# Later sums of weights, attention spills on ScalarE's queue, and four chunks first in a two-layer diffusion block

## The chip, the cores and the metric

One Trainium2 chip, one of its cores. The metric is the device time of one execution in microseconds, the median of several runs. TensorE (PE) multiplies, ScalarE (ACT) and VectorE (DVE) work elementwise, GpSimd (POOL) and SyncE (SP) mostly issue DMAs here. Each engine takes its instructions strictly in the order in which the program has them.

## The reference, cut to what matters

512 latent tokens and 256 context tokens of width 1024 go through two layers, in float32. A layer is

```python
h = modulate(rms_norm(x, norm1_g[l]), sh1, sc1)
glu, q, k, v, rq, rk, rv, rg, gates = split(h @ w_in[l] + b_in[l])
a   = conv_module(glu, ...)                    # depthwise convolution of 31 taps, layer norm
att = latent_attention(q, k, v, k_c, v_c)      # 8 heads, 2 key/value heads
ret = retention_output(bidir_retention(rq, rk, rv, ...), rg, ...)
y   = merge_branches(gates, a, att, ret, w_pa, w_pb, w_pc) @ w_out[l]
x   = x + g1 * y
gt, val = split(modulate(rms_norm(x, norm2_g[l]), sh2, sc2) @ w_up[l])
x   = x + g2 * ((silu(dwconv(gt)) * val) @ w_down[l])
```

The context tokens take the same path in layer 0 only (768 tokens there, 512 in layer 1). sh, sc and g come from the conditioning through `w_ada`.

## The kernel before

**Products.** A float32 operand is split into a high and a low part (`whi`, `wlo` for weights, `hh`, `hl` for activations), and a block of 128x128 weights takes three matmuls: `hh,whi`, `hl,whi`, `hh,wlo`. Weights come as one stream of tiles `raw` of 512 KB or less, loaded on SP's queue (L199, six buffers); ACT makes `whi` of each (L218), DVE `wlo` (L219).

**Feed-forward of layer 0.** `w_up` is not multiplied as it stands. For each of 22 chunks (`c`) the four blocks 11, 12, 21, 22 are combined in seven products on half of the tokens (384): 11, 12, S2, S1, S3, 22, S4. S1 to S4 are sums of the weights' blocks. They are made in DRAM, in six batches of four chunks (the last of two), by `make_sums`: per batch four copies (L627, 1 MB each, half of it in the last batch) and four accumulating DMAs (L632), all issued by POOL. Of a batch S1 = 21 + 22, S3 = 11 + 21, S2 = 11 + S1, S4 = 12 + S2, so that an S2 waits for an S1 and an S4 for an S2. `make_sums` is called after six steps of `ORDER[0]`, named in `SUMAT`, with a whole batch each; only its four copies have a dependency on the last matmul of the step.

**The mixers.** `ORDER` gives the steps of a layer: K, Q0, R0 and so on. Attention (`mixers`) runs beside them in four units of two heads each. A unit scores in PSUM tiles `ps`, takes exponentials on ACT (`prob`, L1361), turns them by PE (L1378), copies them to SBUF on ACT (`probt`, L1379), multiplies by `vt` (tile `ps<-probt,vt`), and leaves its result in a tile `att` (ACT, L1393). A complete `att` is written to DRAM (`attsp`) by `spill` (L1497) on POOL's queue, since nearly all tiles share 45 slots of SBUF; its slot can be used again when the write has landed. After the attention one load on POOL's queue (L1583) brings `ij`, from which retention's decay tables are made (`kdec` L916, `dec` L930 on ACT, and DVE behind them), and `kb` (L981).

**POOL's order.** In layer 0 the queue holds, one behind the other: sums, spills of attention, the load of `ij`, and behind the last sum the loads of `rowa` (L588) and `crow` (L574), with which DVE computes modulations (`crowt` L577, L599).

**From the mixers to the feed-forward.** `last_chunks` multiplies by `w_out`, the last four output chunks on one half of the tokens and then on the other. While the second half runs, the generator `split_tokens` advances the norm of the first half, a fixed number of steps per chunk. `up_seven` then begins with the products 11 and 12 of chunks 0 to `UPFIRST`-1, which need the first half alone. S2 needs both halves: the norm's `rstd`, then on DVE `b` (L708), `t` (L744, L745), then `hh` on ACT (L716) and `hl` on DVE (L717). ACT and DVE evacuate the products into `fg` (L1732, L1737) in the same stretch.

Of the kernel before, what the change touches and what calls it, by code (L numbers as in the profile page):

```python
# [18 lines left out]
F32 = mybir.dt.float32  # L19
F32R = mybir.dt.float32r  # L20
AF = mybir.ActivationFunctionType
ALU = mybir.AluOpType
# [3 lines left out]
P = 128  # L26
D = 1024
KC = D // P
# [9 lines left out]
NUP = 74  # L38
# [8 lines left out]
ORDER = ('K Q0 R0 Q1 A R1 G0 C G1 G2 G3 P0 P1 P2 P3 T T T T',  # L47
         'K Q0 Q1 R0 A G0 C R1 G1 G2 G3 P0 P1 P2 P3 T T T T T T')
ATT_LEAD, RET_LEAD = (3, 2), (1, 1)
ATTR, RETR, CONVR, ADAR = (1.0, 1.0), (1.4, 1.6), (0.4, 0.4), (0.06, 0.28, 0.4, 0.33)  # L50
SUMAT = ("R1", "G1", "G2", "G3", "P1", "P2")
QLAG = 2
HOLDO, HOLDD = (4, 4), (4, 6)
LEADO, LEADD, LEADB = 2, 2, ((0, 0, 0), (4, 0, 4))
# [15 lines left out]
HALF = TALL // 2  # L70
EVEN = [(0, HALF), (HALF, HALF)]
Q = 4 * P
# [22 lines left out]

UPFIRST = 3
CUTS = ((0, 4), (4, 8), (8, 12), (12, 16), (16, NFF))
CUTAT = {5: 0, 9: 1, 13: 2, 17: 3}  # L100

# [1 line left out]
def up_order():  # L103

    first = range(UPFIRST)
    out = [(n, c) for c in first for n in ("11", "12")] + [(n, c) for n in ("S2", "S1", "S3") for c in first]
    for c in range(UPFIRST - 1):
        out += [("22", c), ("S4", c)]
    for c in range(UPFIRST, NFF):
        out += [("11", c), ("22", c - 1), ("S4", c - 1)]  # L110
        if c in CUTAT:
            out.append((CUTAT[c],))
        out += [("12", c), ("S2", c), ("S1", c), ("S3", c)]
    return out + [("22", NFF - 1), ("S4", NFF - 1)]
# [3 lines left out]
BLOCKS = ("11", "12", "21", "22")  # L118

SUMS = (("S1", "21", ("22",)), ("S3", "11", ("21",)), ("S2", "11", ("S1",)), ("S4", "12", ("S2",)))  # L120


def batches():
    return [range(c, min(c + BATCH, NFF)) for c in range(0, NFF, BATCH)]
# [14 lines left out]
def parts(segs):  # L139

    if len(segs) > 1:
        return [[s] for s in segs]
    n = segs[0][1] // 2
    return [[(0, n)], [(n, n)]]
# [140 lines left out]
class Kern:  # L285
# [90 lines left out]
        self.cost = n * 3 * sum(c for _, c in segs) * 0.000425  # L376
        return pts

    def last_chunks(self, key, xs, segs, hold, evac, norm, lead=0, limit=None):

        n = len(xs)
        if lead:
            for m, pts in enumerate(self.group([lambda k, m=m: key(m, k) for m in range(lead)], xs, segs)):
                evac(m, pts)
            self.tick(self.cost)
        for m in range(lead, KC - hold):
            evac(m, self.dense(lambda k: key(m, k), xs, segs))
            self.tick(self.cost)  # L390
        self.W.keep(P)
        if limit:
            self.W.limit = limit
        ws, tiles = [], []
        for m in range(KC - hold, KC):
            ws.append([])
            for k in range(n):
                ws[-1].append(self.W.next(key(m, k), P))
                if k == 0:
                    tiles.append(self.W.cur)  # L400
        tiles.append(self.W.cur + (self.W.off == SUB))
        gen = None
        halves = parts(segs)[::-1] if limit else parts(segs)
        for i, hs in enumerate(halves):
            for j, m in enumerate(range(KC - hold, KC)):
                evac(m, self.dense(None, xs, hs, ws[j]))
                if i == len(halves) - 1:
                    ws[j] = None
                    self.W.release(tiles[j + 1])
                if gen:  # L410
                    for _ in range(1 + KC // hold):
                        next(gen, None)
                self.tick(self.cost)
            if gen:
                for _ in gen:
                    pass
            gen = norm(hs)
        self.W.release()
        return gen
# [198 lines left out]
        t = self.up_sums[b][name] if name in self.up_sums[b] else self.io[f"wup{4 * b + BLOCKS.index(name)}"]  # L618
        return t[:, j * Q:j * Q + Q]

    def make_sums(self, b):

        n = len(batches()[b]) * Q
        src = {x: self.io[f"wup{4 * b + i}"] for i, x in enumerate(BLOCKS)}
        for name, base, more in SUMS:
            t = src[name] = self.up_sums[b][name] = self.dram.tile([P, n], F32, name=f"sum{name}_{b}")
            first = self.nc.gpsimd.dma_start(t, src[base], max_dma_last_dim=2048)  # L627

            info = mybir.DependencyInfo(mybir.DependencyClass.Sync, mybir.DependencyReason.DATA)
            self.tc.add_manual_dep(first.ins, self.last_mm.ins.name, info, reason="later")  # L630
            for x in more:
                self.nc.gpsimd.dma_start(t, src[x], accum_op=ALU.add, max_dma_last_dim=2048)  # L632


    def rstd2(self, pts, name, y=None):

# [857 lines left out]
            nc.vector.tensor_tensor(merged[m][:, :w], merged[m][:, :w], th[:, :w], op=ALU.add)  # L1494

    def spill(self, dst, t, w):
        self.nc.gpsimd.dma_start(dst[:, :w], t[:, :w])  # L1497

    def reload(self, src, n, w):
        out = []  # L1500
# [54 lines left out]
    def layer_mixers(self, l, last, segs, T, xs, xsp, first, h2):  # L1555
        nc, io = self.nc, self.io
# [11 lines left out]
        def scaled(gen, rate):  # L1568
            for us in gen:
                yield None if us is None else us / rate  # L1570

        def mixers():
            def ready(hp):
                if hp == 0:
                    self.finish(qk["K"], qk["Q0"])
                if hp == 2:
                    self.finish(qk["Q1"])
                self.att_done = hp
            yield from scaled(self.att_gen(nt, ready), ATTR[l])
            self.att_done = 4  # L1580
            self.qq = self.kk = self.vt = None
            self.ij = self.S("ij")
            nc.gpsimd.dma_start(self.ij[:, :4 * P + 2], io["ij"])  # L1583
            self.ret_tables()
            for p in range(4):
                while self.ret_in[p] is None:
                    yield None
                a, self.ret_in[p] = self.ret_in[p], True
                yield from scaled(self.ret_gen(p, *a, not last), RETR[l])
                self.ret_done += 1  # L1590
            self.rvt = self.rv = self.ij = None
        us = [None] * 4
        ths, merged = [], [None] * KC
        for step in ORDER[l].split():
            kind, i = step[0], int(step[1:] or 0)
            if kind == "K":
                qk[step] = self.side(self.kv_unit(first.pop(0) if first else None))
            elif kind == "Q":
                qk[step] = self.side(self.q_unit(i, nt, first.pop(0) if first else None))
            elif kind == "R":  # L1600
                self.rv_unit(i)
            elif kind == "A":
                mix = self.side(mixers())
            elif kind == "G":
                us[i] = self.glu(i, segs, T)
            elif kind == "C":
                conv = self.side(self.conv_gen(us, segs), CONVR[l])
            elif kind == "P":
                while self.att_done < min(4, i + ATT_LEAD[l]) or self.ret_done < i - RET_LEAD[l]:
                    mix.step()  # L1610
                self.ret_in[i] = self.ret_inputs(i, segs, T)
            elif kind == "T":
                ths.append(self.gate(2, len(ths), segs))
            if l == 0 and step in SUMAT:
                self.make_sums(SUMAT.index(step))
        self.finish(mix)
        if l == 0:
            self.finish(ada)
# [26 lines left out]
        def evac(m, pts):  # L1645
            for pt, o, c in kinds(pts):
# [4 lines left out]

        norm = self.norm(l, 1, xs, h2) if last else self.split_tokens(l, xs, h2)
        return self.last_chunks(lambda m, k: ("w_out", l, k * P, m * P), mm, even(segs), HOLDO[l], evac, norm, LEADO,
                                None if l else NUP + UPFIRST)

    def ffn(self, l, h2, xs, segs, T, gen, xsp, xup):
        nc = self.nc
# [56 lines left out]
        def up_seven():  # L1714

            X, Z, g, val = {}, {}, {}, {}
# [22 lines left out]
            def s2_first():  # L1739

                ws = [self.W.next_operand("S2", c) for c in range(UPFIRST)]
                for ks in ((0, 1), (2, 3)):
                    for c in range(UPFIRST):
                        product(X[c], "S2", c, False, ws[c], ks)
# [5 lines left out]
                nc.scalar.activation(g[c][:, two], X[c], AF.Copy)  # L1750

            def s1(c):
                Z[c] = (self.ps() if 0 < c < UPFIRST else self.dps())[:, :HALF]
                product(Z[c], "S1", c)

            def s3(c):
# [25 lines left out]
            steps = {"11": p11, "12": p12, "S2": s2, "S1": s1, "S3": s3, "22": p22, "S4": s4}  # L1782
            ready = {"11", "12"}
            for n, x in enumerate(up_order()):
                if len(x) == 1:
                    down(x[0])
                    continue
                while x[0] not in ready:
                    ready.add(next(gen))
                if x == ("S2", 0):  # L1790
                    self.W.limit = self.W.total
                    s2_first()
                elif x[0] != "S2" or x[1] >= UPFIRST:
                    steps[x[0]](x[1])
                if n == 0:
                    next(gen)
            xs.clear()

# [54 lines left out]
        norm = self.out_norm(xs) if l + 1 == DEPTH else self.norm(l + 1, 0, xs, self.h)  # L1853
# [137 lines left out]
```

## Time and profile before

| | |
|---|---|
| median of 3 runs | 2313.04 us (2312.16 to 2316.35) |
| the profiled execution | 2318.38 us, of it 2316.6 us in the span |
| PE busy | 2232.2 us (96%) |
| DVE, ACT, POOL busy | 1604.8, 989.0, 144.5 us |
| PE's longest waits | 23.9 us at 351.8, 14.7 us at the start, 6.7 us at 869.2 |

Times in the rows are us from the span's start. Where an engine waited before an instruction, the row ends with the length of that wait and what ended it. PE is busy nearly throughout, so a change counts by the gaps between its matmuls and by the stretches in which its granted clock is low.

### The profile page before, as it was taken

How to read it: one execution, taken by the hardware profiler on the slowest of the kernel's cores; microseconds unless marked ns; L12 is line 12 of the kernel's file. 1: busy time of each engine (PE TensorE's matmuls, PEld its weight loads, DVE VectorE, ACT ScalarE, POOL GpSimd, SP SyncE). 2: the span in 40 equal slices, each digit the busy share in tenths (PEclk: the TensorE clock that was granted, in tenths of full speed). 3: DMA queues.
4: the chain of work that ended last, by engine and by line, in shares of the span. 5: the costliest groups of instructions: out<-in, count | busy, mean ns of one | idle time of the engine just before them, and what ended most of it. 6: DMA issues, size and time to landing. Idle time of an engine off the chain costs nothing.

```text
span 2316.6 us, 34409 instructions
## 1 busy us (share of the span) xinstructions
PE 2232.2 (96%) x13386; PEld 2037.1 (88%) x13386; DVE 1604.8 (69%) x3219; ACT 989.0 (43%) x1707; POOL 144.5 (6%) x225
## 2 busy tenths in 40 slices
PE   6999968999999989999999989999999999999998
PEld 5988958999999989999999979888887889888887
DVE  6876936889985567565655669878699756744445
ACT  3465643342242346554454434565343434423233
POOL 0001111100010000101101100000001100000000
PEclk9999989999999999999999999999999999999999
DMA  8226894813343333737647521111126623432221
GB/s 304 101 99 173 232 243 126 216 64 117 129 156 128 106 103 100 182 119 191 153 152 183 184 109 56 58 55 58 55 80 222 252 84 111 159 113 97 100 91 37
DMA packets 104466, 307.03 MB, mean 133 GB/s; under 512 B 11024, under 2 KB 13344, under 8 KB 104304
## 3 DMA queue, kind: packets, MB, share of 16 engines
q1 hardware_dynamic: 66240, 186.34, 23.5%
q0 software_dynamic: 38064, 118.50, 18.9%
q8 instruction: 105, 1.72, 0.3%
q14 instruction: 57, 0.47, 0.1%
HBM read 282.26 MB, written 68.68 MB: 151 GB/s over the span
## 4 chain that ended last, share of the span: by engine, by line
PE 53%; issue 3%; DVE 3%; DMA 1%; ACT 1%; POOL 0%; DVEq 0%; POOLq 0%; ACTq 0%
PE pd L319 31%; PE pd L1724 11%; PE ps L319 8%; PE ps L1724 2%; PE ps L1378 1%; DVE wlo L219 1%; DMA crow<-crow 0%; DMA rowa<-wadt 0%; ACT whi L218 0%; DVE cacc L827 0%; DMA rl<-attsp 0%; DVE qq L1326 0%; ACT dx L1805 0%; DMA raw<-wstream 0%; DVE rowa L599 0%
## 5 line engine op out<-in xcount | busy, mean ns | idle before, releaser
L218 ACT ACTIVATE whi<-raw 128x1024 fp32r<-128x1024 f32 x313 | 331.4, 1061 | 748.0 <-PE pd L319 492.0
L219 DVE TENSOR_TENSOR wlo<-raw,whi 128x1024 fp32r<-128x1024 f32 x313 | 382.3, 1222 | 258.8 <-ACT whi L218 245.1
L319 PE MATMUL pd<-hh,whi 128*128 128x384 f32 (+2 forms) x1472 | 471.1, 360 | 0.0
L319 PE MATMUL pd<-hh,wlo 128*128 128x384 f32 (+2 forms) x1472 | 470.2, 359 | 0.0
L319 PE MATMUL pd<-hl,whi 128*128 128x384 f32 (+2 forms) x1472 | 469.5, 359 | 0.0
L319 PEld LDWEIGHTS pd<-hh,whi 128*128 128x128 f32 x1472 | 270.9, 188 | 28.0 <-issue 1.8
L319 PEld LDWEIGHTS pd<-hh,wlo 128*128 128x128 f32 x1472 | 271.4, 188 | 25.9 <-issue 1.1
L319 PEld LDWEIGHTS pd<-hl,whi 128*128 128x128 f32 x1472 | 271.2, 188 | 25.9 <-issue 0.7
L827 DVE SCALAR_TENSOR_TENSOR cacc<-u,vec,cacc 128x497 f32<-128x497 f32 (+9 forms) x360 | 220.9, 650 | 2.0
L1724 PE MATMUL pd<-hh,whi 128*128 128x384 f32 x512 | 171.8, 339 | 9.1 <-ACT hh L716 9.1
L1724 PE MATMUL pd<-hl,whi 128*128 128x384 f32 x512 | 172.3, 336 | 0.5 <-DVE hl L717 0.4
L1724 PE MATMUL pd<-hh,wlo 128*128 128x384 f32 x512 | 171.7, 336 | 0.0
L1361 ACT ACTIVATE prob<-ps,amx,qrs 128x256 f32<-128x256 f32 (+1 forms) x144 | 93.8, 656 | 91.3 <-DVE amx L1356 74.9
L319 PE MATMUL pd<-whi,hl 128*128 128x256 f32 x416 | 120.3, 290 | 5.9 <-DVE hl L784 5.9
L319 PE MATMUL pd<-whi,hh 128*128 128x256 f32 x416 | 120.3, 292 | 2.1 <-ACT hh L781 2.1
L319 PE MATMUL pd<-wlo,hh 128*128 128x256 f32 x416 | 119.3, 287 | 0.0
L319 PE MATMUL pd<-hidh,whi 128*128 128x512 f32 (+1 forms) x302 | 104.1, 356 | 4.0 <-DVE x L1814 4.0
L1724 PEld LDWEIGHTS pd<-hh,whi 128*128 128x128 f32 x512 | 96.5, 189 | 12.0 <-ACT hh L716 10.1
L319 PE MATMUL pd<-hidl,whi 128*128 128x512 f32 (+1 forms) x302 | 103.1, 353 | 0.0
L319 PE MATMUL pd<-hidh,wlo 128*128 128x512 f32 (+1 forms) x302 | 102.9, 354 | 0.0
L599 DVE SCALAR_TENSOR_TENSOR rowa<-rowa,crow 128x768 f32<-128x768 f32 (+1 forms) x144 | 94.4, 686 | 8.9 <-DMA rowa<-wadt 8.9
L588 POOL DMA_DIRECT2D rowa<-wadt x72 | 39.1, 543 | 950.1 <-DVE wlo L219 737.1
(298 smaller groups left out, 4312.1 us busy)
## 6 DMA issues: line engine op xcount, KB each, us to landing
raw<-wstream SPq DMA_DIRECT2D x236, 512.0 KB, 3.5
rowa<-wadt POOLq DMA_DIRECT2D x72, 512.0 KB, 4.3
sumS<-wup POOLq DMA_DIRECT2D x30, 1024.0 KB, 13.0
raw<-sumS SPq DMA_DIRECT2D x88, 256.0 KB, 3.7
raw<-wup SPq DMA_DIRECT2D x66, 256.0 KB, 3.6
xup<-dx POOLq DMA_DIRECT2D x32, 384.0 KB, 7.2
sumS<-sumS POOLq DMA_DIRECT2D x10, 1024.0 KB, 9.7
adar<-wada SPq DMA_DIRECT2D x16, 384.0 KB, 7.6
```

What stands on the lines that cost most here:

```text
L218: nc.scalar.activation(hi, r, AF.Copy)
L219: nc.vector.tensor_tensor(lo, r, hi.bitcast(F32), op=ALU.subtract)
L319: self.last_mm = self.nc.tensor.matmul(out, w, x, start=start, stop=stop)
L588: nc.gpsimd.dma_start(loaded[-1], self.io["wadt"][l, 8 * pc + c])
L599: nc.vector.scalar_tensor_tensor(out, raw[:, a:b], 1.0, t[:, o:o + b - a], op0=ALU.mult, op1=ALU.mult, accum_out=acc[:, c, j, h:h + 1])
L827: nc.vector.scalar_tensor_tensor(acc[:, a:b], u[:, a + d:b + d], w(k), acc[:, a:b], op0=ALU.mult, op1=ALU.add)
L1361: nc.scalar.activation(pr[:, o - k0:o - k0 + c], pt[:, :c], AF.Exp, scale=rs, bias=mx[:, 2:3], accum_out=sm[:, j:j + 1])
L1378: nc.tensor.transpose(pt[:, b * P:b * P + P], pr[:, o + b * P:o + b * P + P], self.ident)
L1724: nc.tensor.matmul(pt, w[:, b], x, start=start and k == 0 and i == 0, stop=k == 3 and i == 2, skip_group_check=not start)
```

## The change

- `make_sums` is called after every step of layer 0 from the ninth (`SUMFROM = 8`, the step G1). Batch b gets its copies in call b, its S1 and S3 in call b+1, S2 in call b+2, S4 in call b+3. Every one of these DMAs now depends on the step's last matmul.
- `spill` issues on ACT's queue (eight writes, four per layer), and `ij` is loaded on SP's queue (two loads).
- `UPFIRST` is 4. The first products come as 11 of four chunks, 12 of four chunks, then S2, S1, S3. In layer 0 the norm advances by 3, 3, 1, 1 steps instead of 3 each, and its next step comes one product later.

```diff
-SUMAT = ("R1", "G1", "G2", "G3", "P1", "P2")
+SUMFROM = 8
...
-UPFIRST = 3
+PACE = (3, 3, 1, 1)
+UPFIRST = 4
...
-    out = [(n, c) for c in first for n in ("11", "12")] + [(n, c) for n in ("S2", "S1", "S3") for c in first]
+    out = [(n, c) for n in ("11", "12", "S2", "S1", "S3") for c in first]
...
-                    for _ in range(1 + KC // hold):
+                    for _ in range(pace[j] if pace else 1 + KC // hold):
...
-    def make_sums(self, b):
+    def make_sums(self, n):
...
+        steps = ((), ("S1", "S3"), ("S2",), ("S4",))
+        for b in range(len(batches())):
+            if not 0 <= n - b < len(steps):
+                continue
...
+                if n == b:
+                    t = sums[name] = self.dram.tile([P, len(batches()[b]) * Q], F32, name=f"sum{name}_{b}")
+                    ops.append(nc.gpsimd.dma_start(t, src[base], max_dma_last_dim=2048))
+                elif name in steps[n - b]:
+                    for x in more:
+                        ops.append(nc.gpsimd.dma_start(sums[name], src[x] if x in src else sums[x], accum_op=ALU.add,
+                                                       max_dma_last_dim=2048))
+            for op in ops:
+                self.tc.add_manual_dep(op.ins, self.last_mm.ins.name, info, reason="later")
...
-        self.nc.gpsimd.dma_start(dst[:, :w], t[:, :w])
+        self.nc.scalar.dma_start(dst[:, :w], t[:, :w])
...
-            nc.gpsimd.dma_start(self.ij[:, :4 * P + 2], io["ij"])
+            nc.sync.dma_start(self.ij[:, :4 * P + 2], io["ij"])
...
-            if l == 0 and step in SUMAT:
-                self.make_sums(SUMAT.index(step))
+            if l == 0 and n >= SUMFROM:
+                self.make_sums(n - SUMFROM)
...
-                                None if l else NUP + UPFIRST)
+                                None if l else NUP + UPFIRST, None if l else PACE)
...
-                Z[c] = (self.ps() if 0 < c < UPFIRST else self.dps())[:, :HALF]
+                Z[c] = (self.ps() if c < UPFIRST else self.dps())[:, :HALF]
...
-                if n == 0:
+                if n == 1:
                     next(gen)
```

**Place 1, the third spill.** POOL's queue before; `sumS2_3` is the sum S2 of batch 3, `attsp2` the third unit's place in DRAM:

```order
L632 DMA sumS1_3_3433<-wup15 512x512
L627 DMA sumS3_3_3436<-wup12 512x512
L627 DMA sumS2_3_3439<-wup12 512x512
L632 DMA sumS3_3_3436<-wup14 512x512
L632 DMA sumS2_3_3439<-sumS1_3_3433 512x512
L627 DMA sumS4_3_3442<-wup13 512x512
L1497 DMA attsp2_104<-att_483_3067 128x768
L632 DMA sumS4_3_3442<-sumS2_3_3439 512x512
L1583 DMA ij_646_3988<-ij 128x514
L1497 DMA attsp3_105<-att_590_3712 128x768
```

ACT's queue of the changed kernel, around the same spill:

```order
L1390 ACTIVATE probt_566_3541<-ps_567_3542 128x512
L1390 ACTIVATE probt_566_3541<-ps_568_3548 128x256
L1404 ACTIVATE att_483_3051<-ps_569_3552 128x128
L1508 DMA attsp2_104<-att_483_3051 128x768
L1372 ACTIVATE prob_574_3570,asm_573_3566<-ps_570_3559,amx_572_3565,qrs_118_830 128x512
L1372 ACTIVATE prob_574_3570,asm_573_3566<-ps_571_3560,amx_572_3565,qrs_118_830 128x256
```

The spill stood behind three accumulating sums, `ij` behind a fourth; now the spill stands right behind the last write to its tile.

**Place 2, the end of the sums.** POOL's queue in the changed kernel, the last sums and what follows them:

```order
L641 DMA sumS4_4_4325<-sumS2_4_4323 512x512
L641 DMA sumS2_5_4658<-sumS1_5_4654 256x512
L641 DMA sumS4_5_4660<-sumS2_5_4658 256x512
L589 DMA rowa0_2_0_5620<-wadt 128x1024
L589 DMA rowa0_2_1_5623<-wadt 128x1024
L575 DMA crow_810_5432<-crow 128x768
```

What follows the last sum is the same as before; all 48 sums still stand ahead of it, and they now begin later.

**Place 3, from `w_out` to `up_seven`.** DVE before, from the norm's last part to the first operand of S2 (`t2_1099`):

```order
L643 SCALAR_TENSOR_TENSOR rstdt_1086_8400<-ps_1085_8397,rstd_1039_7808 128x384
L1737 TENSOR_TENSOR fg_1083_8382<-fg_1083_8382,ps_1087_8405 128x384
L644 TENSOR_TENSOR rstdt_1086_8400<-rstdt_1086_8400,rstd_1039_7808 128x384
L1737 TENSOR_TENSOR fg_1089_8420<-fg_1089_8420,ps_1091_8435 128x384
L645 SCALAR_TENSOR_TENSOR rstd_1039_7808<-rstdt_1086_8400,rstd_1039_7808 128x384
L219 TENSOR_TENSOR wlo78_8529<-raw78_8522,whi78_8528 128x1024
...
L219 TENSOR_TENSOR wlo79_8536<-raw79_8525,whi79_8535 128x1024
L744 TENSOR_TENSOR t3_1098_8489<-b_1097_8484,b_1096_8479 128x768
L219 TENSOR_TENSOR wlo80_8543<-raw80_8532,whi80_8542 128x1024
L745 SCALAR_TENSOR_TENSOR t2_1099_8490<-t3_1098_8489,b_1064_8227 128x768
```

and in the changed kernel (`t2_1103`):

```order
L220 TENSOR_TENSOR wlo78_8556<-raw78_8552,whi78_8555 128x1024
L728 TENSOR_TENSOR hl_1081_8377<-b_1079_8367,hh_1080_8376 128x768
L654 SCALAR_TENSOR_TENSOR rstdt_1089_8423<-ps_1088_8420,rstd_1039_7808 128x384
L655 TENSOR_TENSOR rstdt_1089_8423<-rstdt_1089_8423,rstd_1039_7808 128x384
L656 SCALAR_TENSOR_TENSOR rstd_1039_7808<-rstdt_1089_8423,rstd_1039_7808 128x384
...
L220 TENSOR_TENSOR wlo80_8573<-raw80_8562,whi80_8572 128x1024
L1748 TENSOR_TENSOR fg_1091_8429<-fg_1091_8429,ps_1098_8488 128x384
L756 SCALAR_TENSOR_TENSOR t2_1103_8527<-t3_1102_8526,b_1064_8227 128x768
L1748 TENSOR_TENSOR fg_1094_8445<-fg_1094_8445,ps_1099_8502 128x384
L220 TENSOR_TENSOR wlo81_8580<-raw81_8569,whi81_8579 128x1024
L728 TENSOR_TENSOR hl_1105_8531<-t2_1103_8527,hh_1104_8530 128x768
```

`wlo78` has moved ahead of the norm's `rstdt`, the three steps of `rstd` stand together, and a fourth `fg` and a `wlo81` stand between `t2` and `hl`.

ACT in the changed kernel, in the same stretch:

```order
L1743 ACTIVATE fg_1094_8445<-pd_1093_8444 128x384
L721 ACTIVATE b_1100_8516<-b_1100_8516,mod0_85 128x384 x2
L721 ACTIVATE b_1101_8521<-b_1101_8521,mod0_85 128x384 x2
L219 ACTIVATE whi80_8572<-raw80_8562 128x1024
L219 ACTIVATE whi81_8579<-raw81_8569 128x1024
L727 ACTIVATE hh_1104_8530<-t2_1103_8527 128x768
```

Before, three `b` stood between `whi80` and `hh` and `whi81` came after it; now `whi80` and `whi81` stand right ahead of `hh`.

## Rows read from the trace of the kernel before

**Rows 1.** The page: busy time, share of the span, instructions
```profile
PE 2232.2 (96%) x13386; PEld 2037.1 (88%) x13386; DVE 1604.8 (69%) x3219; ACT 989.0 (43%) x1707; POOL 144.5 (6%) x225
```

**Rows 2.** Waits of PE, whole execution: us in total, times, longest
```profile
PE ps L319 <- ACT probt L1379: 23.9, 1, 23.9
...
PE pd L1724 <- ACT hh L716: 9.1, 3, 6.7
```

**Rows 3.** Timeline of PE, 322 to 370 us: start, length, instruction, [idle before]
```profile
351.79 1.98 PE L319 MATMUL ps<-probt,vt 128*64 128x128 f32 x16 [23.90 <-ACT probt L1379]
...
364.90 1.59 PE L319 MATMUL ps<-rq,rk 64*128 64x128 f32 x8 [3.45 <-DVE kb L981]
```

**Rows 4.** Timeline of ACT, 294 to 366 us
```profile
296.02 0.30 ACT L1393 ACTIVATE att<-ps 128x128 f32<-128x128 f32 x1
...
326.27 0.21 ACT L1361 ACTIVATION_READ_ACCUMULATOR prob<-ps,amx,qrs 128x1 f32 x1
351.35 0.38 ACT L1379 ACTIVATE probt<-ps 128x256 f32<-128x256 f32 x1 [24.87 <-DMA attsp<-att]
...
361.00 0.49 ACT L916 ACTIVATE kdec<-lg,ij 128x8 f32<-128x8 f32 x2 [6.91 <-DMA ij<-ij]
```

**Rows 5.** Timeline of POOL, 296 to 372 us
```profile
334.25 1.04 POOL L632 DMA_DIRECT2D sumS<-wup  x1 [14.76 <-DMA sumS<-wup]
...
337.75 0.96 POOL L1497 DMA_DIRECT2D attsp<-att  x1
...
351.50 0.99 POOL L1583 DMA_DIRECT2D ij<-ij  x1
```

**Rows 6.** DMA, 289 to 328 us: queue (packets, MB, share), issues (us to landing)
```profile
q0 software_dynamic: 3126, 7.75, 90.3%
...
raw<-wstream SPq DMA_DIRECT2D x3, 512.0 KB, 7.6
```

**Rows 7.** The same, 328 to 352 us
```profile
q0 software_dynamic: 2158, 6.03, 95.3%
...
attsp<-att POOLq DMA_DIRECT2D x1, 384.0 KB, 13.5
```

**Rows 8.** Stretches: us, busy of PE, PEld, DVE, ACT, POOL, PEclk, DMA
```profile
350.00:355.00 5.00, 3.21 (x20) 2.88 (x21) 0.00 (x0) 1.66 (x6) 2.20 (x3) 0.52 0.51 92
365.00:370.00 5.00, 5.00 (x30) 4.72 (x31) 3.55 (x7) 0.12 (x1) 0.00 (x0) 0.66 0.00 0
867.00:874.00 7.00, 4.84 (x16) 4.66 (x17) 5.37 (x9) 3.04 (x5) 0.00 (x0) 0.52 0.39 134
900.00:945.00 45.00, 45.00 (x258) 44.33 (x257) 34.47 (x47) 27.91 (x36) 1.59 (x3) 1.00 0.41 135
```

**Rows 9.** Timeline of POOL, first and last sums from G1 on, and crow
```profile
232.26 1.29 POOL L627 DMA_DIRECT2D sumS<-wup  x2 [24.42 <-PE ps L1378]
...
456.09 0.87 POOL L632 DMA_DIRECT2D sumS<-sumS  x1 [7.88 <-DMA sumS<-sumS]
...
512.62 1.61 POOL L574 DMA_DIRECT2D crow<-crow  x3
```

**Rows 10.** Timeline of DVE, 515 to 560 us
```profile
519.73 0.56 DVE L577 TENSOR_SCALAR crowt<-crowt 128x768 f32<-128x768 f32 x1 [0.22 <-ACT crowt L576]
```

**Rows 11.** Timeline of PE, 858 to 900 us
```profile
862.17 0.34 PE L1724 MATMUL ps<-hh,wlo 128*128 128x384 f32 x1
869.16 1.33 PE L1724 MATMUL pd<-hh,whi 128*128 128x384 f32 x3 [6.66 <-ACT hh L716]
...
875.78 0.80 PE L1724 MATMUL pd<-hh,whi 128*128 128x384 f32 x3 [1.15 <-ACT hh L716]
```

**Rows 12.** Timeline of ACT, 853 to 896 us
```profile
868.27 0.84 ACT L716 ACTIVATE hh<-t 128x768 fp32r<-128x768 f32 x1 [3.14 <-DVE t L745]
```

**Rows 13.** Timeline of DVE, 853 to 896 us
```profile
857.93 0.56 DVE L643 SCALAR_TENSOR_TENSOR rstdt<-ps,rstd 128x384 f32<-128x384 f32 x1 [1.16 <-ACT rstd L640]
...
867.28 0.95 DVE L745 SCALAR_TENSOR_TENSOR t<-t,b 128x768 f32<-128x768 f32 x1
```

More of the change, by code (lines that the diff above doesn't have):

```diff
@@ L377, in dense, with last_chunks @@
         return pts
-    def last_chunks(self, key, xs, segs, hold, evac, norm, lead=0, limit=None):
+    def last_chunks(self, key, xs, segs, hold, evac, norm, lead=0, limit=None, pace=None):
         n = len(xs)
@@ L619, in up_operand @@
         return t[:, j * Q:j * Q + Q]
-    def make_sums(self, b):
[L623 to L632, printed above, removed]
+    def make_sums(self, n):
+        nc = self.nc
+        info = mybir.DependencyInfo(mybir.DependencyClass.Sync, mybir.DependencyReason.DATA)
+        steps = ((), ("S1", "S3"), ("S2",), ("S4",))
+        for b in range(len(batches())):
+            if not 0 <= n - b < len(steps):
+                continue
+            sums = self.up_sums[b]
+            src = {x: self.io[f"wup{4 * b + i}"] for i, x in enumerate(BLOCKS)}
+            ops = []
+            for name, base, more in SUMS:
+                if n == b:
[7 more added lines that the diff above has]
+                self.tc.add_manual_dep(op.ins, self.last_mm.ins.name, info, reason="later")
     def rstd2(self, pts, name, y=None):
@@ L1593, in layer_mixers @@
         ths, merged = [], [None] * KC
-        for step in ORDER[l].split():
+        for n, step in enumerate(ORDER[l].split()):
             kind, i = step[0], int(step[1:] or 0)
```

## The prediction

> **What bounds the kernel now.** I read the page first: PE is busy for 2232.2 of 2316.6 us [rows 1], so time can only go where PE pauses or runs at a low clock. The second view is the list of PE's waits [rows 2]. Its largest entry is one single wait of 23.9 us for `probt` of ScalarE, and further down stand three waits for `hh`, 9.1 us together. The change is aimed at these two places; I see no other that it touches on PE's path.
>
> The first place. PE stood still for 23.90 us up to 351.79, and again for 3.45 us up to 364.90 [rows 3]. In both cases ACT is the one that PE waits for, directly or through `kb`. ACT's own timeline shows why: it finished a `prob` at 326.48, and its next `probt` began at 351.35 after 24.87 us in which it waited for the DMA of a spill to land [rows 4]. The tile to be spilled had been complete since 296.32 (296.02 + 0.30) [rows 4]. POOL issued the spill at 337.75 only, since a sum in front of it waited 14.76 us for another sum to land [rows 5]. So of the 55 us from a complete tile to a landed one, 41.4 went by in POOL's queue and 13.5 in the transfer [rows 5, 7]. Behind it the load of `ij` left at 351.50 and held `kdec` for 6.91 us [rows 4, 5].
>
> The second place, 862 to 876 us, is the beginning of `up_seven`. PE ends the last product that it has operands for at 862.51, waits 6.65 us, and 1.15 us more at 875.78 [rows 11]. The releaser is `hh`, which waits for `t` of DVE [rows 12]. From 857.93 to 868.23 DVE goes through `rstd`, `b`, `t` and three `wlo` and three `fg` in between, with no idle time between its 13 instructions [rows 13]. This gap is bound by DVE's chain.
>
> **The spill and `ij`.** In the new order the spill stands right behind the ACT instruction that completes its tile, and depends on nothing else. It leaves near 296.5 instead of 337.75. How long a write from ACT's queue takes here no row shows. From below, a load of 512 KB on the SP queue landed in 7.6 us while sums took 90% of the DMA engines [rows 6]; from above, this same spill took 13.5 us from POOL [rows 7]. It lands at 304 to 310, and its slot is wanted at 326.48. The cover is 16 us even at the long end, and I take the wait as gone. Were the landing to take over 30 us, each us beyond would come back. `ij` goes onto SP's queue ahead of weight loads and has 30 us or more before `kdec`; I set its wait to nothing, too. On ACT eight more issues cost, by POOL's 0.96 us for the same one [rows 5], at most 8 us in an engine that is busy for 43% [rows 1]: nothing on the path.
>
> What the gap is worth: 23.90 + 3.45 = 27.35 us of standing still. PE came out of it at a low clock: 0.52 from 350 to 355, of which PE ran from 351.79 on, and 0.66 from 365 to 370 [rows 8]. 0.52 over five us is half speed until about 354.8, so 3.0 us at half speed lose 1.5 us, and 5 x 0.34 is 1.7 us. With a PE that never stops I count both as recovered: 27.35 + 3.2 = 30.55. Against that stand the short waits for ACT and DVE that attention has between its units anyway and that the long gap now hides; I leave 0.8 us for them (none to 4). **First term: -29.8 us, from -26 to -30.6.**
>
> A rule of the Trainium skill speaks against this term. The rows say that 41.4 of the 55 us were spent before the issue. "DMA: Bandwidth & Descriptors", section "Issuing engines are not separate DMA queues", says that DMAs from any engine share the same 16 DMA engines and that issuing from several saves only the usually small issue time. By the rule alone the first term would be about 1 us; by the rows it is 29.8, since here the queue in front of the issue waits for landings, which is no bandwidth.
>
> **The sums.** Nothing is removed: 40 DMAs of 1 MB and 8 of half that, 44 full ones, now start at G1 (232.26 in the trace [rows 9]) rather than at 168. POOL's queue has no spill in it any more, and what stands behind the last sum are `rowa` and `crow`. Price of a sum: from 328 to 352, with no other traffic but one spill, 6.03 - 0.39 = 5.64 MB, or 5.4 sums of 1.05 MB, passed in 24 us: 4.5 us each [rows 7]. From 289 to 328, with weights beside them, 7.75 MB or 7.4 sums in 39 us: 5.3 us each [rows 6]. From 232.26 to 456.09 [rows 9] the 36 that were left took 224 us, 6.2 us each, but this includes a pause of some 30 us with nothing due. I take 5.3, the one with PE and the weight loads at work; 4.5 and 6.2 are the bounds. With about 10 us of an empty queue between the first two steps (an estimate: only four copies are due at first), the last sum is done at 232 + 10 + 44 x 5.3 = 475.
>
> When is it too late? `crow` was issued at 512.62 and taken by DVE at 519.73 [rows 9, 10], 7.1 us later. All later steps come 29.8 us earlier, so DVE will want `crow` near 490 and POOL has to be through by 483. At 5.3 us it is, with 8 us to spare: **second term 0**. At 4.5 us nothing changes either, since the last sums wait for their step of PE. At 6.2 us the last is done at 515 and `crow` is 32 us late; DVE's queue holds `wlo` of the coming weights behind it, so PE would starve after the few us of split weights that it has in hand: 27 us.
>
> **Four chunks first.** PE gets 24 more matmuls (11 and 12 of chunk 3, 12 each) before it needs S2. They lie 0.17 us apart here: 24 x 0.173 = 4.2 us of work for the gap of 6.65 us. On DVE's chain to the first `hh` one of the three `wlo` (1.1 us in the chain) is moved ahead of it. But on ACT `hh` now stands behind `whi81`, whose buffer comes free when PE ends a product of chunk 3. By hand I get the first S2 at 868.4 in place of 869.16, and PE idle for 2.0 instead of 6.65 us. The next operands come at 875.0 instead of 875.78, with 30 matmuls (5.2 us) more done than before at that point: 0.8 + 5.2 = 6.0 us. From 867 to 874 the clock was 0.52 [rows 8]; what that cost is inside this count, and if the clock falls again in the shorter gaps, about 1.7 us (as after 364.90) go back. Later, from 900 to 945, PE is busy for 45.00 of 45 us [rows 8]; there the new chunk order asks more of ACT and DVE close together, which can cost up to 4 us, or nothing. **Third term: -5.5 us, from -1 to -8.** The norm's pace is part of this chain and gets no price of its own.
>
> **The sum.** On the profiled execution, 2318.4 - 29.8 - 5.5 = 2283.1 us. It lies 5.3 us above the median of the runs, 2313.0, which gives 2277.7; I say 2278.
>
> **Rivals.**
> - **Only the stall goes.** The gap at 862 is DVE's chain and moves with it: the chunks' extra `fg`, `wlo81` and `whi81` take what the 24 matmuls cover, or the waits reappear behind 900. 2313 - 29.8 + 0 to 2 = 2283 to 2285. For it: DVE has no idle time there [rows 13]; against it: PE's extra work does not depend on that chain.
> - **Part of the stall stays.** ACT gets its slot, but PE meets a late `ij`, late weights under sums that keep the DMA engines full, or DVE's decay tables. At 10 us or so of new waits: 2288 to 2298.
> - **The spill lands as late as before,** the rule cited above worked out here: the 16 engines have been at 90 to 95% with sums since 289 [rows 6, 7], and whoever issues, the data waits until they are through. Then only 1 us of issue and the join's 5.5 go: 2306 to 2307. Against it: weights landed in 7.6 us in just that stretch [rows 6].
> - **The sums end too late, slower than before.** POOL takes its queue in order, and `crow` stands behind all 44. The cost is 242 + 44 x r - 488 us for a price of r each (483, and 5 us that PE has in hand). At r = 6.4 it takes up the 35 us gained; at 6.5 it is 40 us, 2318 us, and every tenth more adds 4.4. For it: they start 64 us later and are more densely packed; against it: 6.2 was reached only with a long pause counted in.
>
> **How the numbers follow.** Forecast with both gains (2270 to 2283) 0.62; only the stall goes 0.19; part of it stays 0.09; the spill as late as before 0.03; sums too late 0.07, of which 0.02 still end faster, 0.01 level and 0.04 slower. About 0.2% (4.6 us) is what a measurement of this kernel can tell from no change. Faster 0.94, same 0.02, slower 0.04. The range from 2271 to 2290 holds the forecast but for its lower end, the second case, and the near end of the third, about 0.8.
>
> **What would show it.** In the trace after: ACT's `probt` without a wait for `attsp`, and PE without a gap over 3 us between 290 and 380; the granted clock at 1.00 in that stretch; the last sum on POOL near 470 to 480 and `crowt` on DVE not waiting for `crow`; at the join one gap of about 2 us and another of 2 to 3. Wrong would be a PE gap whose releaser is `ij`, `raw` or `crow`, a spill that takes over 25 us to land, or PE waits of more than 4 us between 900 and 960 of the old times.

## The result, and the profile after

The changed kernel takes 2287.62 us in the median of 4 runs (2281.46 to 2289.41), the kernel before 2313.11 in the runs beside it: a ratio of 0.9883, interval 0.9861 to 0.9904. Faster, as forecast, and inside the range; but 25.5 us less instead of the 35 of the forecast. The profiled execution took 2288.56 us, 29.8 us less than the one before.

The page first; it answers to [rows 1]. PE is busy for the same time, in a span that is 30.1 us shorter:

```profile
PE 2231.7 (98%) x13386; PEld 2039.5 (89%) x13386; DVE 1604.8 (70%) x3219; ACT 989.1 (43%) x1707; POOL 138.2 (6%) x215
```

PE's waits after, which answer to [rows 2] (us in total, times, longest): `probt` is gone from the list, `hh` is smaller, and two waits for split weights are new.

```profile
PE pd L1735 <- ACT hh L727: 5.6, 3, 2.1
...
PE pd L1735 <- DVE wlo L220: 2.0, 1, 2.0
...
PE pd L1735 <- ACT whi L219: 1.1, 1, 1.1
```

**The stall.** ACT's timeline of the same place as [rows 4]. The `probt` that had waited 24.87 us follows at once, and `kdec` waits 0.40 us, for ACT's own `att` and not for `ij`:

```profile
326.36 0.21 ACT L1372 ACTIVATION_READ_ACCUMULATOR prob<-ps,amx,qrs 128x1 f32 x1
326.45 0.39 ACT L1390 ACTIVATE probt<-ps 128x256 f32<-128x256 f32 x1
...
329.88 0.49 ACT L927 ACTIVATE kdec<-lg,ij 128x8 f32<-128x8 f32 x2 [0.40 <-ACT att L1404]
```

PE is busy for 89.46 of the 90 us from 290 to 380, at a granted clock of 1.00.

The DMA issues of 290 to 350 us after, which answer to [rows 6, 7] (count, size, median us from issue to landing). The spills from ACT's queue landed in 8.0 us, in a stretch in which copies from POOL's queue took 29.6:

```profile
sumS<-wup POOLq DMA_DIRECT2D x10, 1024.0 KB, 29.6
...
attsp<-att ACTq DMA_DIRECT2D x2, 384.0 KB, 8.0
ij<-ij SPq DMA_DIRECT2D x1, 257.0 KB, 3.9
```

**The end of the sums.** POOL's last sums and `crow`, then DVE's `crowt` ([rows 9, 10]). All three are where the prediction put them: the last sum issued by 475, `crow` at 483, DVE at 490 and not waiting for the load. The row at 460.70 shows what set this end: POOL had waited 21.44 us for PE's step.

```profile
460.70 1.91 POOL L641 DMA_DIRECT2D sumS<-sumS  x2 [21.44 <-PE ps L320]
473.36 0.88 POOL L641 DMA_DIRECT2D sumS<-sumS  x1 [10.74 <-issue]
...
482.68 1.60 POOL L575 DMA_DIRECT2D crow<-crow  x3
```

```profile
489.81 0.56 DVE L578 TENSOR_SCALAR crowt<-crowt 128x768 f32<-128x768 f32 x1 [0.22 <-ACT crowt L577]
```

**The join.** PE's timeline after, from the first S2 on ([rows 11]; times are 30 us earlier than before):

```profile
838.14 0.97 PE L1735 MATMUL pd<-hh,whi 128*128 128x384 f32 x4 [1.70 <-ACT hh L727]
...
845.17 0.98 PE L1735 MATMUL pd<-hh,whi 128*128 128x384 f32 x4 [1.87 <-ACT hh L727]
...
868.65 1.54 PE L1735 MATMUL pd<-hh,whi 128*128 128x384 f32 x4 [2.08 <-ACT hh L727]
...
914.05 0.44 PE L1735 MATMUL pd<-hh,whi 128*128 128x384 f32 x1 [1.10 <-ACT whi L219]
...
916.70 0.69 PE L1735 MATMUL pd<-hh,wlo 128*128 128x384 f32 x1 [2.02 <-DVE wlo L220]
```

and stretches of it, in the columns of [rows 8]:

```profile
836.00:842.00 6.00, 3.88 (x21) 3.23 (x20) 5.22 (x8) 3.74 (x6) 0.00 (x0) 1.00 0.56 175
842.00:848.00 6.00, 4.12 (x22) 3.48 (x21) 4.77 (x6) 2.03 (x4) 0.00 (x0) 1.00 0.01 3
...
866.00:872.00 6.00, 3.92 (x14) 3.15 (x13) 4.48 (x6) 4.36 (x6) 0.00 (x0) 0.73 0.40 152
...
914.00:918.00 4.00, 1.92 (x6) 1.60 (x7) 3.51 (x6) 1.30 (x3) 0.75 (x2) 0.82 0.70 247
918.00:922.00 4.00, 4.00 (x20) 4.00 (x19) 1.46 (x2) 3.24 (x8) 1.45 (x2) 0.75 0.58 142
```

The gap of 6.66 us has become one of 1.70, and the clock stays at 1.00 there, where it was 0.52 before. But 75 us later PE waits 1.10 and 2.02 us for `whi` and `wlo`, and twice the granted clock falls to half of full speed for some 3 us. How much is left is read from two events that stand on either side of the feed-forward of layer 0, before and then after: `brh` in the branch projections, and the first product of the last part of `w_down`.

```profile
688.75 0.62 PE L319 MATMUL pd<-brh,whi 128*128 128x384 f32 x2 [0.36 <-ACT brh L448]
...
1337.14 0.78 PE L319 MATMUL pd<-hidh,whi 128*128 128x512 f32 x2 [3.99 <-DVE x L1814]
```

```profile
658.83 0.62 PE L320 MATMUL pd<-brh,whi 128*128 128x384 f32 x2 [0.36 <-ACT brh L449]
...
1306.30 1.01 PE L320 MATMUL pd<-hidh,whi 128*128 128x512 f32 x2 [3.98 <-DVE x L1825]
```

Up to the first event the kernel gained 29.92 us. Between the two it took 648.39 us before and 647.47 after: 0.9 us for the whole join. The traces of the experiments below bear this out: in the seven kernels with the old join the stretch between these two events took 647.60 to 650.08 us, 648.71 in the mean, and in four with the new one (the changed kernel twice, the join alone, the sums two steps later) 647.47 to 648.09, 647.78 in the mean.

### The profile page after: what moved, and what is told of

Read it like the earlier page. It is cut to its first block, busy times and chain, and to the rows that moved or that the text cites. A ratio compares the mean times of both kernels' runs of the same rounds, so it can differ in the third digit from the quotient of the medians.

```text
span 2286.5 us, 34375 instructions
## 1 busy us (share of the span) xinstructions
PE 2231.7 (98%) x13386; PEld 2039.5 (89%) x13386; DVE 1604.8 (70%) x3219; ACT 989.1 (43%) x1707; POOL 138.2 (6%) x215
## 4 chain that ended last, share of the span: by engine, by line
PE 88%; DVE 5%; issue 4%; ACT 1%; DMA 1%; POOL 0%; SPq 0%; DVEq 0%; POOLq 0%; ACTq 0%
PE pd L320 58%; PE ps L320 14%; PE pd L1735 11%; PE ps L1735 3%; PE ps L1389 2%; DVE wlo L220 1%; ACT whi L219 1%; DVE cacc L838 0%; PE ps L1302 0%; DMA rowa<-wadt 0%; DMA x<-xt 0%; DVE qq L1337 0%; DMA rl<-attsp 0%; DVE sq L672 0%; DVE kb L992 0%
## 5 line engine op out<-in xcount | busy, mean ns | idle before, releaser
L320 PEld LDWEIGHTS pd<-hh,whi 128*128 128x128 f32 x1472 | 270.8, 188 | 27.9 <-issue 1.5
L1735 PE MATMUL pd<-hh,whi 128*128 128x384 f32 x496 | 166.8, 341 | 6.8 <-ACT hh L727 5.6
L1735 PE MATMUL pd<-hh,wlo 128*128 128x384 f32 x496 | 167.0, 337 | 2.0 <-DVE wlo L220 2.0
L1735 PE MATMUL pd<-hl,whi 128*128 128x384 f32 x496 | 167.1, 337 | 0.4 <-DVE hl L728 0.4
L600 DVE SCALAR_TENSOR_TENSOR rowa<-rowa,crow 128x768 f32<-128x768 f32 (+1 forms) x144 | 94.3, 686 | 6.1 <-DMA rowa<-wadt 6.1
```

What stands on the lines that cost most here:

```text
L320: self.last_mm = self.nc.tensor.matmul(out, w, x, start=start, stop=stop)
L600: nc.vector.scalar_tensor_tensor(out, raw[:, a:b], 1.0, t[:, o:o + b - a], op0=ALU.mult, op1=ALU.mult, accum_out=acc[:, c, j, h:h + 1])
L1735: nc.tensor.matmul(pt, w[:, b], x, start=start and k == 0 and i == 0, stop=k == 3 and i == 2, skip_group_check=not start)
```

## Experiments: which part takes the stall away

Three theories were open. Q: the spill waited in POOL's in-order queue, and that alone counts. B: the DMA engines are full, and a spill is late whoever issues it. S: the later sums are needed as well. Also open was whether the move of `ij` matters at all, of which the prediction made little.

**Spills and `ij` moved, nothing else.**

```diff
-        self.nc.gpsimd.dma_start(dst[:, :w], t[:, :w])
+        self.nc.scalar.dma_start(dst[:, :w], t[:, :w])
...
-            nc.gpsimd.dma_start(self.ij[:, :4 * P + 2], io["ij"])
+            nc.sync.dma_start(self.ij[:, :4 * P + 2], io["ij"])
```

> The kernel before with only the spills on ACT's queue and ij on SP's; sums and join as before. Theory Q (the spill waited in POOL's in-order queue behind sums that wait for each other): ACT's wait for attsp is gone, 26 to 31 us less, 2282 to 2287 us. Theory B (the DMA engines full of sums are what makes it late, whoever issues): the wait for attsp stays above 10 us, 2300 us or more. Theory S (the later sums are needed as well): somewhere between, 2290 to 2300.

Measured: 2287.45 us, ratio 0.9874 (0.9852 to 0.9895). The whole gain of the change is here, with the sums begun as early as before, so the later sums (S) are not needed for it. B falls too: the third spill landed in 6.5 us and `ij` in 7.8 (the row below), while POOL's queue had the DMA engines busy for 88.8% of the time from 315 to 335 us.

```profile
ij<-ij SPq DMA_DIRECT2D x1, 257.0 KB, 7.8
```

**Later sums alone**, spills and `ij` on POOL as before (the diff of `make_sums` and its call, from the change).

> The kernel before with only the later, spread sums; spills and ij stay on POOL. The third spill then stands behind sums of which none waits for a sum just issued, so theory Q says that it leaves POOL at about 296 and the wait for attsp goes here too; ij stands behind the fourth spill and the sums of the step P0, lands near 340 and costs PE some 8 to 12 us: 2290 to 2296 us. Theory B: the spill lands 13 us or more after 296 but still before 326, the same. A theory that the move to ACT is needed says a wait of 15 us or more for attsp, 2300 us or more.

Measured: 2317.53 us, ratio 0.9995 (0.9985 to 1.0006): no gain at all, and my expectation was wrong. The spill did leave at 296.37, and no `probt` waited for it. But `ij` took the stall over. From this kernel: the issues between 290 and 390 us, then ACT's `kdec`, then PE.

```profile
sumS<-wup POOLq DMA_DIRECT2D x10, 1024.0 KB, 28.4
...
attsp<-att POOLq DMA_DIRECT2D x2, 384.0 KB, 27.9
ij<-ij POOLq DMA_DIRECT2D x1, 257.0 KB, 24.7
```

```profile
367.59 0.49 ACT L927 ACTIVATE kdec<-lg,ij 128x8 f32<-128x8 f32 x2 [22.31 <-DMA ij<-ij]
```

```profile
370.35 1.16 PE L320 MATMUL pd<-hh,whi 128*128 128x384 f32 x2 [25.81 <-ACT rk L1447]
```

`ij`, 257 KB, was under way for 24.7 us, sent from the queue that had just sent four copies of 1 MB; from SP's queue it took 7.8 us in the run above, beside sums in flight.

**Spills alone on ACT**, sums and `ij` as before (the first pair of lines of the diff above).

> The kernel before with only the spills on ACT; ij stays on POOL behind the last sum of batch 3. In the run with both moved that sum left POOL at 348 us, so ij lands near 358 and kdec, due at 330, waits for some 25 to 28 us: theory Q says that the stall only changes its place, 2308 to 2318 us. The theory that the spill alone made the stall says 2283 to 2290 us.

Measured: 2316.71 us, ratio 1.0008 (0.9995 to 1.0021). POOL's timeline and PE's gap:

```profile
350.16 1.00 POOL L632 DMA_DIRECT2D sumS<-sumS  x1 [11.54 <-DMA sumS<-wup]
350.79 0.96 POOL L1583 DMA_DIRECT2D ij<-ij  x1
```

```profile
362.93 1.59 PE L319 MATMUL ps<-rq,rk 64*128 64x128 f32 x8 [27.64 <-DVE kb L981]
```

The gap of 23.90 us at `probt` [rows 3] has gone, and one of 27.64 us stands 7.4 us of work further on (it begins at 335.29, the old one began at 327.89). Two waits were due at nearly the same time. While both are there the first hides most of the second, and taking the first away alone only uncovers the second.

**`ij` alone on SP** (the second pair of lines).

> The kernel before with only ij on SP; sums early, spills on POOL. The wait for attsp of 24 us stays, since the third spill still stands behind sums that wait for each other; only the wait for kb of 3.5 us behind it can go: 2310 to 2316 us, or 0 to 5 us less than the kernel before. If ij alone were the cause: 2283 to 2290 us.

Measured: 2310.61 us, ratio 0.9977 (0.9964 to 0.9989), 3 to 8 us less. The wait for the spill is still there in this kernel's list of waits:

```profile
ACT probt L1379 <- DMA attsp<-att: 25.5, 1, 25.5
```

**Later sums and `ij` on SP, spills on POOL.**

> The later sums with ij on SP, but the spills on POOL. The third spill left POOL at 296.4 in the run with the sums alone and took about 28 us to land behind four copies of 1 MB; its slot is due at 326.5. The theory that POOL's transfers land in turn says a wait for attsp of 0 to 4 us and nearly the whole gain, 2286 to 2293 us. A theory that the move to ACT is needed says 2300 us or more.

Measured: 2286.75 us, ratio 0.9872 (0.9855 to 0.9889). The whole gain, without ACT's queue. The spills of this kernel took up to 30.8 us to land, and `probt` did not wait. The view of the spills (`attsp`):

```profile
DMA to landing us min/median/max: 2.3/4.7/30.8
```

Together the five runs say: the spill has to leave early enough, and for that either the move to ACT or the later sums will do; `ij` has to leave POOL's queue in either case. With the sums alone or the spill alone nothing is gained, with `ij` alone 3 to 8 us.

## Experiments: the price of the sums

**Sums begun two steps later still.**

```diff
-SUMFROM = 8
+SUMFROM = 10
```

> The changed kernel with the sums begun two steps later (G3 instead of G1). By the prediction's price of 5.3 us the last S2 is issued near 535, crow right behind it, 45 to 50 us after DVE wants it: 2322 to 2340 us, with DVE waiting for crow. A theory that the sums' end does not reach PE (DVE's queue and PE have enough in hand) says under 2300 us.

Measured: 2325.82 us, ratio 1.0043 (1.0029 to 1.0056), 38 us more than the changed kernel. Here `crow` is issued at 516.37 on POOL, DVE gets on at 527.96, and PE has a gap of 28.83 us (and one of 6.11 before it):

```profile
516.37 0.90 POOL L575 DMA_DIRECT2D crow<-crow  x1
```

```profile
527.96 0.56 DVE L578 TENSOR_SCALAR crowt<-crowt 128x768 f32<-128x768 f32 x1 [31.21 <-ACT crowt L577]
```

```profile
531.98 1.15 PE L320 MATMUL pd<-hh,whi 128*128 128x384 f32 x2 [28.83 <-DVE mrg L1499]
```

So the prediction's slower rival is a real mechanism: `crow` left 33 us after 483, the rival's sum makes that 28 us of PE's time (33 less the 5 in hand), and the gap that ends behind it is 28.83 us. The 6.11 us before it are not a wait for `crow`: DVE was busy without a pause there, with `mrg` behind 7.78 us of the convolution's `cacc` in its queue; why this kernel has that order was not looked into. The 535 of the expectation was late by 19 us. From 400 to 515 us POOL's queue had the DMA engines busy for 99.9% of the time and moved 25.82 MB, 24.6 sums of 1.05 MB in 115 us, so that a sum's price under this load was 4.7 us and not 5.3.

## Experiments: the join

**The join's part alone**, on the kernel before, and **the changed kernel without it** (`UPFIRST` and the lines below it in the change, added or taken back).

> The kernel before with only UPFIRST 4, the products' order and the norm's pace. The prediction's third term says 5.5 us less, 2307.5 us. The trace of the changed kernel (events behind the join moved by 0.9 us only, with a new pair of waits of 3.1 us and a low clock some 75 us after the join) says 0 to 2 us less, 2311 to 2313 us.

> The changed kernel without UPFIRST 4, the products' order and the pace. The prediction's third term says 5.5 us more than the changed kernel, 2293 us; the trace says 0 to 2 us more, 2287 to 2290 us, with the old gap of 6.7 us back at the join and no waits of 1 to 2 us for wlo and whi behind it.

Measured: 2316.4 us, ratio 0.999 (0.9975 to 1.0004), and 2289.61 us, ratio 0.988 (0.9856 to 0.9904). The changed kernel was run again beside later experiments:

> The changed kernel itself once more, beside the next ones on the same chip: 2286 to 2289 us.

It took 2286.81 us. By these medians the part brings something between nothing and some 3 us; their intervals alone would not rule out 5.5 (that of the join's part alone reaches 5.8 us less). The traces do: 0.9 us between the two events above, in the mean as in the first pair.

**Why: a buffer's turn.** The program gives split weights four buffers, so tile 96 takes the buffer of tile 92. PE's order of the changed kernel, at the partial product of `w_down` (tile 92) in chunk 5:

```
L320 MATMUL ps_1164_9193<-hidl_1146_9015,whi92_9032 128x384
L320 MATMUL ps_1163_9192<-hidh_1145_9014,wlo92_9033 128x384
L320 MATMUL ps_1164_9193<-hidh_1145_9014,wlo92_9033 128x384
L1735 MATMUL pd_1149_9084<-hh_1104_8530,whi96_9230 128x384
L1735 MATMUL pd_1149_9084<-hl_1105_8531,whi96_9230 128x384
L1735 MATMUL pd_1149_9084<-hh_1104_8530,wlo96_9231 128x384
```

Nothing stands between the last use of tile 92 and the first of tile 96. ACT and DVE can split tile 96 only then, and DVE has 2.1 us of `fy` in front of it. ACT's row and DVE's row for tile 96:

```profile
912.96 1.04 ACT L219 ACTIVATE whi<-raw 128x1024 fp32r<-128x1024 f32 x1
```

```profile
915.43 1.22 DVE L220 TENSOR_TENSOR wlo<-raw,whi 128x1024 fp32r<-128x1024 f32 x1
```

A kernel that puts the partial product between 11 and 22 of its chunk has no such pair:

```diff
-        out += [("11", c), ("22", c - 1), ("S4", c - 1)]
+        out.append(("11", c))
         if c in CUTAT:
             out.append((CUTAT[c],))
-        out += [("12", c), ("S2", c), ("S1", c), ("S3", c)]
+        out += [("22", c - 1), ("S4", c - 1), ("12", c), ("S2", c), ("S1", c), ("S3", c)]
```

> The changed kernel with the partial product of w_down put between 11 and 22 of its chunk instead of behind S4. In PE's order no product then stands right behind the last use of the buffer that its own weights need (0 matmuls between tile 92 and tile 96 in the changed kernel). The theory that this reuse makes the pair of waits at 914 to 917 us says that both go, with the low clock behind them: 3 to 5 us less than the changed kernel in the same trace, 2282 to 2285 us. A theory that ACT and DVE are too busy there says that waits of 2 to 4 us stay: 2286 to 2290 us.

Measured: 2286.01 us, ratio 0.9869 (0.9854 to 0.9884). Both waits are gone from its trace, so the buffer's turn made them. But the 3 to 5 us did not come: the time is that of the changed kernel within its spread. A wait of nearly their size stands at the same place, for `dx` of ACT, which stood behind a `crowt` that waited for a load on POOL's queue:

```profile
916.22 1.31 PE L320 MATMUL ps<-hidh,whi 128*128 128x384 f32 x2 [2.87 <-ACT dx L1816]
```

```profile
914.86 0.84 ACT L577 ACTIVATE crowt<-crow 128x768 f32<-128x768 f32 x1 [7.25 <-DMA crow<-crow]
```

**The loads of `crow` ahead of their use**, on top of this, by 3.6 and by 10 us of the count by which the program spaces its steps:

```diff
                 nc.gpsimd.dma_start(t[:, :w], self.io["crow"][:, o:o + w])
+            yield 3.6
+            for t, o, w in zip(self.crow, (0, TALL, 2 * TALL), (TALL, TALL, 512)):
                 th = self.S("crowt")
```

> The kernel with the early partial product, and the three loads of crow issued together one step ahead of their use. In the run with the early partial product ACT waited 7.25 us for a load of crow ahead of dx, and PE 2.9 us for that dx, with the low clock behind it. The theory that this is all that is left behind the join says that the wait goes: 2280 to 2283 us. A theory that every such repair only moves the wait says no change, 2285 to 2288 us.

> The same with crow loaded some 10 us ahead of its use instead of 3.6. By the first theory the same or a little less than the run before, 2280 to 2283 us; by the second 2285 to 2288 us.

Measured: 2285.2 us (ratio 0.9867, 0.9852 to 0.9881) and 2291.33 us (0.9893, 0.9877 to 0.991), the second outside both of its expectations. In the first, the stretch that held the waits is clean, PE busy for 20.00 of 20 us at a clock of 1.00 (first row below). Yet PE then waits longer at the end of the feed-forward, 3.98 us in the changed kernel and 6.43 here, in the second 13.78:

```profile
905.00:925.00 20.00, 20.00 (x118) 20.00 (x117) 6.72 (x7) 10.69 (x22) 7.07 (x9) 1.00 0.90 210
```

```profile
1304.17 1.01 PE L320 MATMUL pd<-hidh,whi 128*128 128x512 f32 x2 [6.43 <-DVE x L1827]
```

```profile
1309.56 1.01 PE L320 MATMUL pd<-hidh,whi 128*128 128x512 f32 x2 [13.78 <-DVE x L1827]
```

That wait is for DVE. `x` stands in its queue behind the products of `rowa` with `crow` (L600, L602 in these two kernels), from which the modulation is computed, and DVE is busy without a pause from those products to `x`. DVE's time in them from 1284 to 1310 us (the views' last lines), in the changed kernel and in these two:

```profile
sum 26.00, DVE 4.98; mean DVE 2.49
sum 26.00, DVE 7.43; mean DVE 3.71
sum 26.00, DVE 14.78; mean DVE 7.39
```

They grow by 2.45 and 9.80 us, and PE's wait grows by 2.45 and 9.80. POOL's queue holds the loads of `rowa` behind those of `crow`, and more of them come late: one is issued between 1270 and 1300 us in the changed kernel, two and five here. That the moved loads of `crow` delay them is read from the order of the queue. No version that is clearly faster than the changed kernel came out: 2285.2 and 2286.0 against 2286.81 lie within the spread of each. The repairs took their waits away, and each time another, next in line, took most of what they gave.

## Why the prediction was right, and where not

**First term, -29.8 us: right.** 29.92 us were gained up to `brh`. The rival that the spill lands as late as before fell: 8.0 us from ACT. A spill took 27.9 us from POOL's queue behind four copies and 8.0 from ACT's beside them, so the queue decides the landing too, and not the issue alone. The Trainium skill's rule in "DMA: Bandwidth & Descriptors", section "Issuing engines are not separate DMA queues", that issuing elsewhere saves only issue time, does not describe this case. The same page of the Trainium skill, section "Queues, rings and completion order", says that a DMA engine takes turns between the queues that have work for it. That fits: a transfer then waits for what its own queue sent earlier and only shares with the others; no run here shows the turns themselves.

**What I had not seen in it:** `ij` is not a rider on this term; without its move the term is nothing (2316.71 us). The trace of before shows 3.45 us of PE's time for it [rows 3], and the run with the spill alone shows 27.64. I did put its wait to nothing for the right reason (SP's queue), but did not ask what each move is worth alone. Nor did I see that the later sums would have freed the spill by themselves.

**Second term, 0: right, but the working met 475 by luck.** I got it as 44 sums at 5.3 us each. In the trace the price did not set the end: POOL waited 17.64 to 35.33 us for PE before every step's sums but the first, and the last sums left when their step of PE let them, as I had it for a price of 4.5 only. The cost of sums that do end late came out as worked out, 28.83 us for 28.

**Third term, -5.5 us: wrong, -0.9.** The join itself went as worked out, somewhat better: gaps of 1.70 and 1.87 us where I had 2.0 and 2 to 3, at full clock. The step that failed is the sentence on 900 to 945, "can cost up to 4 us, or nothing", of which I took 0.5 into the sum. It cost 1.10 + 2.02 us of waiting and, by the clocks of 914 to 922 shown above, up to 1.7 us of low clock behind them. The wait of 2.08 at 868.65 was 1.31 in the trace before, and the low clock behind it in this trace, up to 1.6 us, is new. The cause of the first two waits could have been read from the order ahead of any run: tile 96 directly behind tile 92. What the join would bring with all of this out of the way stays open, since no version showed it in the time.

**The step from the profile to the median** failed too. I took 5.3 us off since the profiled execution lay so far above three runs. The later runs of the kernel before have medians of 2315.95 to 2317.95 (2309 to 2324), and the changed kernel's profiled execution lies only 0.9 us above its median. Trace against trace gives 29.8 us, the second set of the changed kernel 29.1 (2286.81 against 2315.95). Of the 9.9 us between 2277.7 and 2287.62, 4.6 are the join's, 4.4 this step's, and 1.0 was lost in the trace behind the second event; the first term gave 0.1 back.

**The rivals.** The case to which I gave 0.62, both gains, did not come; the time fell inside the range because the range took in the rivals. "Only the stall goes" (0.19) is what happened in effect; its 2283 to 2285 was too low by most of the 4.4 us of the base, and it named the place, waits behind 900, that gave the join's gain back. My sign for such waits, more than 4 us, was set too wide: 3.12 us and the low clock were enough. "Sums too late" was not near here, but the run with `SUMFROM = 10` shows it at 2325.82. Two slips changed nothing: the cases add up to 0.95 for faster and 0.01 for the same, not 0.94 and 0.02, and DVE's 13 rows before S2 are 15 instructions.

## What to carry to other kernels

When a trace shows one long wait at an in-order queue, look for everything else that goes through the same queue and is due soon after: the next one is hidden behind the first, and the first alone may be worth nothing. Small transfers that someone waits for should not share an issuing queue with megabytes of background copies, neither for the issue nor for the landing. And where work is moved ahead into a gap, look in the order for buffers that come round: a product directly behind the last use of the buffer that its own operand needs has to wait for the split in between, and can give the gain back.

## What the runs showed of the hardware

In these runs a transfer landed behind what its own queue had sent before it, and shared with what other queues had sent. 384 KB took 27.9 us from POOL behind four copies of 1 MB, and 8.0 from ACT beside such copies. 257 KB took 24.7 us from POOL behind four copies, and 7.8 from SP beside sums in flight (the 3.9 from SP in the changed kernel came as the DMA engines ran empty).

A pause of PE of some 2 us can be followed by a granted clock at half of full speed for some 3 us, which costs up to 1.7 us more, and is not always. In the profiled execution it followed the waits of 2.08 and 2.02 us (0.73 from 866 to 872, 0.75 from 918 to 922) and not that of 1.87 (1.00 from 842 to 848). In the same kernel's second trace it followed 1.86 us (the row below) and not 2.08 (1.00 from 866 to 872), so the length of the pause alone does not decide it.

```profile
842.00:848.00 6.00, 5.17 (x21) 5.13 (x21) 4.43 (x5) 3.16 (x5) 0.00 (x0) 0.72 0.01 3
```

How much of the difference between two executions of one kernel comes from this is not shown.
